# A two-layer hybrid encoder trunk: another order of the mixer's threads, and norms of two tiles in shared steps

## The chip, the cores and the metric

The kernel runs on one core of one Trainium2 chip. The metric is the device time of one execution in microseconds. The engines are named as the profile names them: PE (matrix multiplication; PEld is its loading of weights), DVE (elementwise, reductions), ACT (activation functions, copies), POOL and SP (here almost only transfers).

## What is computed

Two layers; in each a half-weighted feed-forward block, a mixer of three parts side by side, and a second feed-forward block, each behind a norm that is shifted and scaled by a conditioning vector. 256 rows (two tiles of 128), 1024 columns, float32.

```python
def dsa_attention(q, k, v, qi, ki, wi):          # queries in two blocks of 128, key chunks of 64
    # per block of queries: 8 index heads of 32
    s = einsum('bqhd,bsd->bqhs', qib, ki) * IDX_DIM ** -0.5
    idx_score = einsum('bqhs,bqh->bqs', relu(s), wib * IDX_HEADS ** -0.5)
    idx_score = where(admissible, idx_score, -inf)       # key chunk <= query chunk
    _, sel = lax.top_k(idx_score, 64)
    logits = einsum('bqhd,bqkd->bqhk', qb, k[sel]) * ATT_HEAD_DIM ** -0.5    # 8 heads of 64
    p = softmax(where(valid, logits, -inf)); o = einsum('bqhk,bqkd->bqhd', p, v[sel])

def s5_mixer(u, ...):            # 16 groups of 16 channels, 64 complex diagonal states each
    x = associative_scan(x_t = A_bar x_{t-1} + B_bar u_t)
    y = gelu(re(C x) + d_skip * u); a, g = split(y @ w_glu); return a * sigmoid(g)

def conformer_conv(h, w_dw, b_dw, ln_g, ln_b, w_pw):
    a, g = split(h); u = a * sigmoid(g)
    y = causal depthwise convolution of u, 31 taps, + b_dw
    return silu(layer_norm(y, ln_g, ln_b)) @ w_pw

def hybrid_mixer(h, w_in, w_out, ...):
    q, k, v, qi, ki, wi, u_ssm, u_conv = split(h @ w_in)
    merged = concatenate([rms_norm(dsa_attention(q, k, v, qi, ki, wi)),   # 512 columns
                          rms_norm(s5_mixer(u_ssm)),                      # 256
                          rms_norm(conformer_conv(u_conv))])              # 256
    return merged @ w_out

def reference(x, c, ...):
    for l in range(2):           # sh, sc, g: nine rows of silu(c) @ mod_w[l] + mod_b[l]
        x = x + 0.5 * g1 * swiglu_ffn(modulate(rms_norm(x), sh1, sc1), ffn1_w_gu[l], ffn1_w_down[l])
        x = x + g2 * hybrid_mixer(modulate(rms_norm(x), sh2, sc2), ...)
        x = x + 0.5 * g3 * swiglu_ffn(modulate(rms_norm(x), sh3, sc3), ffn2_w_gu[l], ffn2_w_down[l])
    return rms_norm(x, final_norm)
```

## The kernel before

Every weight matrix streams from memory once. `Stream` loads it in units of 128 x 1024 floats (`raw`) and splits each unit into a high part (ACT, L102) and a low part (DVE, L106), `hi` and `lo`; PE then makes three products per block (`mm3`, L330 to L332). Six `hi`/`lo` pairs exist; a new unit's split is issued when an older unit is done with (`st.done()`).

The feed-forward blocks are long, dense runs of such products. The mixer, which the change is about, is eight threads written as Python generators: `W` is the input projection (10 steps: tiles A, C, four of B, four of Q, which land in `ps_in`, `ps_kT`, `ps_inC`, `ps_inB`, `ps_inQ`), `K` copies keys and index queries out, `I` and `J` are the index scores and the top-k of the first and of the second tile of queries (`ps_idx`, `rl`, `idx`, then `maskb`), `S` is the state-space part (`ps_U`, `ps_V`, the scan, `ps_Y`, `ps_yT`, `ps_glu`, `ps_sg`), `C` the convolution part (`uT`, its shifted copy `U4` made by four transfers, `ps_cv`, a layer norm with `ps_cy` and `ps_cyT`, `ps_pw`), and `a` and `b` are the attention proper of the first and of the second tile (`qT`, logits `ps_lg`, softmax `Pm`, transposes `ps_PT`, products `ps_o` and `osb`). Each part's result is normed, transposed back into `ps_mg` or `ps_sg`, and split into `xTh` (ACT) and `xTl` (DVE) by `merged`; the output projection (`ps_y`) reads these. Its units come in the order of columns 4 to 7, then 0 to 3: state-space, convolution, attention.

The table `MIX_ORDER` says in which order the threads' steps are written down. A planner then places each engine's instructions in one fixed row, by readiness in its own estimate and by the order written, and every engine takes its row strictly in turn: an instruction whose operand is late holds all that stand behind it. The PSUM banks are few: two each in `ps_g` and `ps_m`, four named ones (`abank`). In the trace the profile's program names leave numbers out; `U` is both the state-space input and `U4`.

A norm needs 1/sqrt of a column of 128 values. `rsqrt_col` makes it on DVE in one guess and two refinements of three instructions each, 128x1.

## Time before, and its profile

| | us |
|---|---|
| median of 3 runs | 1192.59 |
| lowest and highest | 1190.36 and 1197.93 |
| the profiled execution | 1190.66 |
| its span, first to last instruction | 1188.9 |
| PE busy in the span | 1099.9 |
| DVE busy | 904.3 |
| ACT busy | 572.3 |
| mixer of the first layer, first input product to last output product | 286.8 to 421.8 |
| mixer of the second layer | 850.5 to 985.6 |

Times within the execution count from the span's start. 1.76 us of the profiled execution's time lie around its span. Busy shares are an average over stages; the mixers are 270 us of the span and hold all but a few instructions of the change.

### The profile page before, as it was taken

The numbers are of one execution on the slowest core, as the hardware profiler recorded it, in microseconds if no ns is written. First come the engines' busy times: TensorE is split into PE (matmuls) and PEld (weight loads), VectorE is DVE, ScalarE is ACT, GpSimd is POOL, SyncE is SP. The second block draws the span as 40 slices with busy tenths as digits, with TensorE's granted clock in tenths as the row PEclk, the third lists the DMA queues.
The fourth block names the chain that finished last, engine by engine and source line by source line (L and its number), as shares of the span: only waits on it lengthen the run. The fifth ranks groups of instructions, "written<-read, shape, count | busy, mean of one in ns | idle before, by whom it ended". The sixth has DMA issues, their size and how long they took to land. (4 is left out here: it accounts for less than half of the span.)

```text
span 1188.9 us, 19063 instructions
## 1 busy us (share of the span) xinstructions
PE 1099.9 (93%) x6915; PEld 941.3 (79%) x6915; DVE 904.3 (76%) x1806; ACT 572.3 (48%) x1032; POOL 119.2 (10%) x160
## 2 busy tenths in 40 slices
PE   3679999987989989999997999999898999999997
PEld 2558887865966869989995888888797687999986
DVE  7678999897775788898757789887677587655655
ACT  4245454445625666645445444444463566544442
POOL 7452001201012000000100000100000000000000
PEclk9789999898987999999899999999989799999999
DMA  9788988786562248678672999998456223767651
GB/s 222 188 275 278 357 290 274 234 290 182 156 147 76 72 131 301 225 236 289 205 230 89 297 330 353 318 327 263 142 156 146 69 80 120 260 198 229 199 175 54
DMA packets 189710, 251.59 MB, mean 212 GB/s; under 512 B 18886, under 2 KB 139906, under 8 KB 189616
## 3 DMA queue, kind: packets, MB, share of 16 engines
q1 hardware_dynamic: 181920, 240.56, 63.5%
q0 software_dynamic: 4704, 7.60, 2.9%
q10 hardware_dynamic: 2992, 2.22, 1.0%
q8 instruction: 54, 0.88, 0.3%
q14 instruction: 40, 0.33, 0.1%
HBM read 245.19 MB, written 1.11 MB: 207 GB/s over the span
## 5 line engine op out<-in xcount | busy, mean ns | idle before, releaser
L102 ACT ACTIVATE hi<-raw 128x1024 fp32r<-128x1024 f32 (+1 forms) x314 | 328.6, 1055 | 329.4 <-PE ps_gt L331 108.1
L106 DVE TENSOR_TENSOR lo<-raw,hi 128x1024 fp32r<-128x1024 f32 (+2 forms) x297 | 359.4, 1216 | 104.6 <-ACT hi L102 99.9
L330 PE MATMUL ps_gt<-xTh,hi 128*128 128x256 f32 x1120 | 319.0, 287 | 3.0 <-DVE h L715 2.4
L332 PE MATMUL ps_gt<-xTh,lo 128*128 128x256 f32 x1120 | 316.1, 286 | 2.2 <-DVE lo L106 2.2
L331 PE MATMUL ps_gt<-xTl,hi 128*128 128x256 f32 x1120 | 317.7, 285 | 0.0
L330 PEld LDWEIGHTS ps_gt<-xTh,hi 128*128 128x128 f32 x1120 | 215.8, 193 | 17.5 <-issue 5.9
L332 PEld LDWEIGHTS ps_gt<-xTh,lo 128*128 128x128 f32 x1120 | 215.1, 193 | 8.7 <-issue 5.0
L331 PEld LDWEIGHTS ps_gt<-xTl,hi 128*128 128x128 f32 x1120 | 216.4, 193 | 2.5 <-issue 1.7
L367 DVE SCALAR_TENSOR_TENSOR macc<-raw,cond,macc 128x512 f32<-128x512 f32 x224 | 167.0, 750 | 26.2 <-DMA raw<-in_mod_w_dram 24.8
L331 PE MATMUL ps_y<-lo,hTh 128*128 128x512 f32 x352 | 141.3, 402 | 5.2 <-DVE lo L106 5.2
L332 PE MATMUL ps_y<-hi,hTl 128*128 128x512 f32 x352 | 140.2, 398 | 1.1 <-DVE hTl L719 1.1
L330 PE MATMUL ps_y<-hi,hTh 128*128 128x512 f32 x352 | 136.4, 399 | 2.5 <-ACT hi L102 2.0
L396 POOL DMA_DIRECT2D spill<-mrow x32 | 16.2, 508 | 683.0 <-ACT mrow L393 573.4
L331 PEld LDWEIGHTS ps_y<-lo,hTh 128*128 128x128 f32 x352 | 67.9, 193 | 21.1 <-DVE lo L106 7.6
L330 PEld LDWEIGHTS ps_y<-hi,hTh 128*128 128x128 f32 x352 | 67.1, 191 | 18.2 <-ACT hi L102 3.1
L332 PEld LDWEIGHTS ps_y<-hi,hTl 128*128 128x128 f32 x352 | 67.8, 193 | 16.3 <-DVE hTl L719 1.9
L713 ACT ACTIVATE silu<-ps_gt 128x256 f32<-128x256 f32 x70 | 25.5, 377 | 50.3 <-PE ps_gt L332 49.9
L330 PE MATMUL ps_gu<-hi,xTh 128*128 128x512 f32 x96 | 40.1, 417 | 6.7 <-DVE xTh L326 6.7
L106 POOL TENSOR_TENSOR lo<-raw,hi 128x1024 fp32r<-128x1024 f32 x17 | 41.8, 2472 | 31.4 <-ACT hi L102 31.4
L332 PE MATMUL ps_gu<-hi,xTl 128*128 128x512 f32 x96 | 40.1, 417 | 3.0 <-DVE xTl L327 3.0
L715 DVE TENSOR_TENSOR h<-silu,ps_gt 128x256 f32<-128x256 f32 x70 | 28.6, 419 | 16.8 <-ACT silu L713 16.8
L331 PE MATMUL ps_gu<-lo,xTh 128*128 128x512 f32 x96 | 39.4, 410 | 0.0
(382 smaller groups left out, 1691.6 us busy)
## 6 DMA issues: line engine op xcount, KB each, us to landing
raw<-in_ffn_w_gu_dram SPq DMA_DIRECT2D x140, 512.0 KB
raw<-in_mod_w_dram SPq DMA_DIRECT2D x128, 512.0 KB
raw<-in_ffn_w_down_dram SPq DMA_DIRECT2D x88, 512.0 KB
raw<-in_ffn_w_gu_dram SPq DMA_DIRECT2D x72, 256.0 KB
raw<-in_w_in_dram SPq DMA_DIRECT2D x20, 512.0 KB
raw<-in_mod_w_dram SPq DMA_DIRECT2D x32, 256.0 KB
raw<-in_w_out_dram SPq DMA_DIRECT2D x16, 512.0 KB
row<-spill POOLq DMA_DIRECT2D x6, 512.0 KB, 4.3
```

Source lines behind the costliest of these rows:

```text
L102: nc.scalar.activation(hi[:, :n], raw[:, :n], AF.Copy)
L106: e.tensor_sub(lo[:, :n], raw[:, :n], hi[:, :n].bitcast(F32))
L330: return [nc.tensor.matmul(ps, xh, wh, start=start, stop=False), nc.tensor.matmul(ps, xh, wl, start=False, stop=False), nc.tensor.matmul(p ...
L331: nc.tensor.matmul(ps, xh, wl, start=False, stop=False),
L332: nc.tensor.matmul(ps, xl, wh, start=False, stop=stop)]
L367: nc.vector.scalar_tensor_tensor(acc, raw[:, 512 * i:512 * i + 512], cond[:, k:k + 1], prev, op0=ALU.mult, op1=ALU.add)
L396: nc.gpsimd.dma_start(d[:, 512 * h:512 * h + 512], r[32 * h:32 * h + 1, :])
L713: nc.scalar.activation(s, ps[i][:, :256], AF.Silu)
L715: nc.vector.tensor_mul(h, s, ps[i][:, 256:])
```

## The change

The table of the mixer is another one. The second tile's index scores and top-k (`J`) are written ahead of the first's (`I`), the second tile's logits (`b`) ahead of the first's (`a`) and ahead of the convolution's products, and the last steps of the state-space and convolution parts behind the attention's. The table-load for the exponential is issued after the second tile's last index scores in place of next to the keys. The two C units count as done only when `qiT` has been copied, and the splits of the units that follow are held behind that copy. The copies of `UU` are held behind the index work. `Tp`'s clearing keeps its written place. The norms of two tiles at the end of `S`, in the layer norm and at the end of `C` are made with one `rsqrt_cols` on 128x2 in place of two `rsqrt_col` on 128x1: it has four instructions in a refinement.

```diff
--- before.py
+++ after.py
@@ -44,9 +44,9 @@
 
 
 MIX_ORDER = """
-W K S K K W K J I J J I W I S J S I W I J J I S W I J I J S W C C C I J J I S W
-I J I J S I J C S W W C S W a b S N a C a C S S b b a C a b C b a a b b b C b b
-b
+W K K S K W K
+J J W J J I W J J I I S W J J I S W J J C C C W J J J S I I W I I S I I S W I I I S S W
+b a b b b b C S a a S b b C b b C S a a b a C b a C S C C
 """
 
 
@@ -265,6 +265,34 @@
             y = y2
             s = 8.0 / 3.0 * s ** 5
         return y
+
+    def rsqrt_cols(v):
+
+        def col2(tag):
+            return sm_p.tile([P, 2], F32, tag=tag, name=tag)
+        y = col2("rs2_y")
+        s = (8.0 / 3.0) ** (-6.0 / 25.0)
+        magic = float(0x5F3759DF) + math.log2(s) * float(1 << 23)
+        nc.vector.tensor_scalar(y.bitcast(I32), v.bitcast(I32), -0.5, magic, op0=ALU.mult, op1=ALU.add)
+        for _ in range(2):
+            a, b, y2 = col2("rs2_a"), col2("rs2_b"), col2("rs2_y")
+            nc.vector.tensor_mul(a, y, v)
+            nc.vector.tensor_mul(a, a, y)
+            nc.vector.scalar_tensor_tensor(b, a, -10.0 / 3.0 * s * s, a, op0=ALU.add, op1=ALU.mult)
+            nc.vector.scalar_tensor_tensor(y2, b, 5.0 * s ** 4, y, op0=ALU.add, op1=ALU.mult)
+            y = y2
+            s = 8.0 / 3.0 * s ** 5
+        return y
+
+    def rms_cols(pair, n, scale=1.0):
+
+        ss = sm_p.tile([P, 2], F32, tag="ss", name="ss")
+        for i, a in enumerate(pair):
+            j = sm_p.tile([P, 512], BF16, tag="junk", name="junk", bufs=1)
+            nc.scalar.activation(j[:, :a.shape[-1]], a, AF.Square, scale=scale * n ** -0.5, accum_out=ss[:, i:i + 1])
+        ms = sm_p.tile([P, 2], F32, tag="ms2", name="ms2")
+        nc.vector.tensor_scalar_add(ms, ss, EPS)
+        return rsqrt_cols(ms)
 
     hold = {}
 
@@ -1053,7 +1081,7 @@
                          wcol[:, n0:n0 + 16].rearrange("p (n o) -> p n o", o=1).to_broadcast([P, 16, 32]))
             yield
         Tp = T("Tp", [8, G, GC])
-        e.memset(Tp, 0.0)
+        tc.keep_in_program_order(e.memset(Tp, 0.0))
         for a in range(8):
             r = GC * (7 - a)
             nc.gpsimd.dma_start(Tp[0:P - r, a], Km[r:P])
@@ -1123,8 +1151,6 @@
                             wh, wl = us[k // 4]
                             cs = slice(256 * (k % 4) + P * j, 256 * (k % 4) + P * j + P)
                             mm3(pin["C"][:, 256 * j:256 * j + 256], wh[:, cs], wl[:, cs], *xT(k), k == 0, k == 7)
-                            if j and k % 4 == 3:
-                                st.done()
                     yield
                 else:
                     pin[i] = [bank(ps_g, f"ps_in{i}") for _ in range(2)]
@@ -1144,10 +1170,6 @@
                 ps = pin["A"][t]
                 nc.scalar.activation(vsb[:, t, :], ps[:, 8:72], AF.Copy)
                 nc.vector.tensor_scalar_mul(wis[:, t, :], ps[:, 0:8], 8 ** -0.5)
-                if t == 0:
-
-                    scr = sm_p.tile([P, 8], F32, tag="scr", name="scr", bufs=1)
-                    nc.scalar.activation(scr, ps[:, 0:8], AF.Exp)
                 yield
             pk = pin["K"][:, :256]
             for e in range(2):
@@ -1155,9 +1177,11 @@
             for b in range(4):
                 (nc.vector.tensor_copy if b % 2 else nc.scalar.copy)(kiT[32 * b:32 * b + 32], pk[64:96])
             for e in range(2):
-                nc.vector.tensor_sub(kTl[64 * e:64 * e + 64], pk[0:64], kTh[0:64].bitcast(F32))
-            yield
-            nc.scalar.activation(qiT, pin["C"], AF.Copy)
+                ktl = nc.vector.tensor_sub(kTl[64 * e:64 * e + 64], pk[0:64], kTh[0:64].bitcast(F32))
+            yield
+            st.after_hi, st.after_lo = (nc.scalar.activation(qiT, pin["C"], AF.Copy),), (ktl,)
+            st.done(2)
+            st.after_hi = st.after_lo = ()
             yield
 
         def att_index(t):
@@ -1170,14 +1194,19 @@
                     nc.tensor.matmul(ps[:, nk * i:nk * i + nk], qiT[32 * b:32 * b + 32, 256 * i + P * t:256 * i + P * t + P],
                                      kiT[32 * b:32 * b + 32, :nk], start=True, stop=True)
                 rl = s2([P, 512], "rl")
-                nc.scalar.activation(rl[:, :2 * nk], ps[:, :2 * nk], AF.Relu, scale=32 ** -0.5)
+                hold["rl"] = nc.scalar.activation(rl[:, :2 * nk], ps[:, :2 * nk], AF.Relu, scale=32 ** -0.5)
                 for i in range(2):
                     h = b + 4 * i
                     if h == 0:
                         nc.vector.tensor_scalar_mul(idx[:, :nk], rl[:, :nk], wis[:, t, 0:1])
                     else:
-                        nc.vector.scalar_tensor_tensor(idx[:, :nk], rl[:, nk * i:nk * i + nk], wis[:, t, h:h + 1],
-                                                       idx[:, :nk], op0=ALU.mult, op1=ALU.add)
+                        hold["idx"] = nc.vector.scalar_tensor_tensor(
+                            idx[:, :nk], rl[:, nk * i:nk * i + nk], wis[:, t, h:h + 1], idx[:, :nk], op0=ALU.mult, op1=ALU.add)
+                if t == 1 and b == 3:
+
+                    scr = sm_p.tile([P, 8], F32, tag="scr", name="scr", bufs=1)
+                    with tc.issue_after(hold["rl"].ins):
+                        nc.scalar.activation(scr, wis[:, 1, :], AF.Exp)
                 yield
             nc.vector.memset(idx[0:64, nk - 64:nk], NEG_INADM)
             for r in range(8):
@@ -1257,8 +1286,9 @@
             yield
             Ug = UU[32:32 + NCH, :].rearrange("c (g a j) -> c g a j", g=G, a=8)
             Ub4 = Ub.rearrange("c a (g j) -> c g a j", g=G)
-            nc.vector.tensor_copy(Ug[:, 0:8], Ub4[:, 0:8])
-            nc.scalar.activation(Ug[:, 8:16], Ub4[:, 8:16], AF.Copy)
+            with st.behind([hold["rl"], hold["idx"]]):
+                nc.vector.tensor_copy(Ug[:, 0:8], Ub4[:, 0:8])
+                nc.scalar.activation(Ug[:, 8:16], Ub4[:, 8:16], AF.Copy)
             ps = abank(0, "ps_U")
             for g in range(G):
                 nc.tensor.transpose(ps[:, NCH * g:NCH * g + NCH], Ug[:, g].rearrange("c a j -> c (a j)"), ident[32:32 + NCH, 32:32 + NCH])
@@ -1343,9 +1373,10 @@
                 nc.scalar.activation(th, pg[e][:, 256:512], AF.Tanh, scale=0.5)
                 s = s1([P, 256], F32, "ss_", "s")
                 nc.vector.scalar_tensor_tensor(s, th, 1.0, pg[e][:, 0:256], op0=ALU.add, op1=ALU.mult)
-                rs = rms_col([s], 256, 0.5)
-                nc.vector.tensor_scalar(s, s, rs, 0.5, op0=ALU.mult, op1=ALU.mult)
                 sp.append(s)
+            rs = rms_cols(sp, 256, 0.5)
+            for e in range(2):
+                nc.vector.tensor_scalar(sp[e], sp[e], rs[:, e:e + 1], 0.5, op0=ALU.mult, op1=ALU.mult)
             yield
             pt = bank(ps_m, "ps_sg")
             v = pt.rearrange("p (k n a e) -> p k e a n", k=2, a=4, e=2)
@@ -1382,20 +1413,21 @@
                 nc.scalar.activation(ya[:, ct, :], pc[:, 256 * ct:256 * ct + 256], AF.Identity, bias=col_a[:, cb + ct:cb + ct + 1])
             yield
             cg, cl = offs["ln_g"] + 2 * l, offs["ln_b"] + 2 * l
-            yn, z_ = {}, {}
+            yn, z_, pts = {}, {}, {}
+            mv = sm_p.tile([P, 2, 2], F32, tag="mv", name="mv")
             for t in range(2):
-                pt = bank(ps_m, "ps_cy")
+                pts[t] = bank(ps_m, "ps_cy")
                 for ct in range(2):
-                    nc.tensor.transpose(pt[:, P * ct:P * ct + P], ya[:, ct, P * t:P * t + P], ident)
+                    nc.tensor.transpose(pts[t][:, P * ct:P * ct + P], ya[:, ct, P * t:P * t + P], ident)
                 bs = sm_p.tile([P, 6], F32, tag="bs", name="bs")
-                mv = sm_p.tile([P, 2], F32, tag="mv", name="mv")
-                nc.vector.bn_stats(bs, pt[:, :256])
-                nc.vector.bn_aggr(mv, bs)
-                v = sm_p.tile([P, 1], F32, tag="ms", name="cv")
-                nc.vector.tensor_scalar_add(v, mv[:, 1:2], EPS)
-                rs = rsqrt_col(v)
+                nc.vector.bn_stats(bs, pts[t][:, :256])
+                nc.vector.bn_aggr(mv[:, t, :], bs)
+            v = sm_p.tile([P, 2], F32, tag="ms2", name="cv")
+            nc.vector.tensor_scalar_add(v.rearrange("p (t o) -> p t o", o=1), mv[:, :, 1:2], EPS)
+            rs = rsqrt_cols(v)
+            for t in range(2):
                 yn[t] = s1([P, 256], F32, "yn", "c")
-                nc.vector.tensor_scalar(yn[t], pt[:, :256], mv[:, 0:1], rs, op0=ALU.subtract, op1=ALU.mult)
+                nc.vector.tensor_scalar(yn[t], pts[t][:, :256], mv[:, t, 0:1], rs[:, t:t + 1], op0=ALU.subtract, op1=ALU.mult)
             yield
             for t in range(2):
                 pt = bank(ps_m, "ps_cyT")
@@ -1420,10 +1452,10 @@
                     mm3(pw[:, 256 * t:256 * t + 256], zh[:, ct, :], zl[:, ct, :], wp[0][:, cs], wp[1][:, cs], ct == 0, ct == 1)
             st.done()
             yield
+            rs = rms_cols([pw[:, 256 * t:256 * t + 256] for t in range(2)], 256)
             for t in range(2):
-                rs = rms_col([pw[:, 256 * t:256 * t + 256]], 256)
                 cm = s1([P, 256], F32, "cm", "c")
-                nc.vector.tensor_scalar_mul(cm, pw[:, 256 * t:256 * t + 256], rs)
+                nc.vector.tensor_scalar_mul(cm, pw[:, 256 * t:256 * t + 256], rs[:, t:t + 1])
                 merge(t, cm, 6, 2)
                 yield
 
```

What this does to the engines' rows, at three places of the first layer's mixer. The second layer's differ from these by a few neighbours.

First, PE where the convolution (`ps_cv`) stands. Before, among the last products of the query projection (`ps_inQ`), with 23 of them behind it:

```order
L330 MATMUL ps_inQ<-xTh,hi 128x256
L1375 MATMUL ps_cv<-U_3419,sl_W_2399 32x256 x64
L1325 MATMUL ps_yT<-ident,ye 128x4x32 x4
L331 MATMUL ps_inQ<-xTl,hi 128x256
L332 MATMUL ps_inQ<-xTh,lo 128x256
```

After, behind the whole projection, in pieces of 5, 6, 3, 5, 17, 11 and 17 among the second tile's logits (tiles 3670 and 3681 are two of its four banks):

```order
L1245 MATMUL ps_lg_3670<-maskb_3446,identb_90 128x256
L1245 LDWEIGHTS identb_90
L1245 MATMUL ps_lg_3681<-maskb_3446,identb_90 128x256
L1406 MATMUL ps_cv_3692<-U4_3403,sl_W4_2399 32x256 x5
L1335 MATMUL ps_Y_3549<-sl_O_1625,X_3506 32x128 x4
L1331 MATMUL ps_Y_3549<-sl_Tp_2474,U_3296 32x128 x4
```

The convolution moved from ahead of all logits to among them, and the last state-space products (`ps_Y`) came behind the projection too.

Second, PE at the start of the output projection (`ps_y00` is the first tile's left half; `ps_o_4093` the second tile's attention products). Before:

```order
L332 MATMUL ps_pw_3975<-hi_3653,zl_3871 128x256
L330 MATMUL ps_y00_4203<-hi_3697,xTh_112 128x512
L331 MATMUL ps_y00_4203<-lo_3698,xTh_112 128x512
L332 MATMUL ps_y00_4203<-hi_3697,xTl_113 128x512
L1239 MATMUL ps_o_4093<-vsb_2973,PT_4110 128x64 x4
L1234 MATMUL ps_PT_4155<-ident_85,Pm_3935 128x128 x4
L1239 MATMUL ps_o_4093<-vsb_2973,PT_4121 128x64 x4
L330 MATMUL ps_y00_4203<-hi_3733,xTh_112 128x512
```

After (`ps_mg_4056` holds the second tile's attention, `ps_mg_4069` the first's; all six groups of `ps_o` stand ahead of this piece):

```order
L360 MATMUL ps_pw_4082<-hi_3535,zl_4053 128x256
L1115 MATMUL ps_mg_4056<-ident_85,osb_3984 128x128 x4
L1115 MATMUL ps_mg_4069<-ident_85,osb_4006 128x128 x4
L1385 MATMUL ps_sg_4102<-ident_85,ss__3928 128x4x32 x2
L1385 MATMUL ps_sg_4102<-ident_85,ss__3932 128x4x32 x2
L358 MATMUL ps_y00_4158<-hi_3618,xTh_112 128x512
L359 MATMUL ps_y00_4158<-lo_3619,xTh_112 128x512
L358 MATMUL ps_y01_4159<-hi_3618,xTh_112 128x512
```

The output products, which were mixed with the attention's, now stand behind all of it, behind both attention transposes and the state-space transposes.

Third, ACT at the same place. Before, the merges of the state-space part (`xTh<-ps_sg`) stand among the attention's copies:

```order
L287 ACTIVATE zh_3870<-czz_3863 128x256
L1092 ACTIVATE xTh_112<-ps_sg_3922,ncol_107 128x128
L1236 ACTIVATE PT_4110<-ps_PT_4105 128x512
L1236 ACTIVATE PT_4121<-ps_PT_4116 128x512
L1092 ACTIVATE xTh_112<-ps_sg_3922,ncol_107 128x128
L277 ACTIVATE junk_4018,ss_4017<-ps_pw_3975 128x256
L102 ACTIVATE hi_4238<-raw_3657 128x1024
L277 ACTIVATE junk_4059,ss_4058<-osb_4056 128x512
```

After, they stand behind seven merges of the attention, and these behind the squares of both `osb` and of `ps_pw`:

```order
L305 ACTIVATE junk_3987,ss_3986<-osb_3984 128x512
L305 ACTIVATE junk_4009,ss_4008<-osb_4006 128x512
L315 ACTIVATE zh_4052<-czz_4045 128x256
L292 ACTIVATE junk_4116,ss_4115<-ps_pw_4082 128x256
L102 ACTIVATE hi_4193<-raw_3539 128x1024
L292 ACTIVATE junk_4118,ss_4115<-ps_pw_4082 128x256
L1120 ACTIVATE xTh_112<-ps_mg_4056,ncol_107 128x128 x3
L1120 ACTIVATE xTh_112<-ps_mg_4069,ncol_107 128x128
L1120 ACTIVATE xTh_112<-ps_mg_4056,ncol_107 128x128
L1120 ACTIVATE xTh_112<-ps_mg_4069,ncol_107 128x128 x2
L1120 ACTIVATE xTh_112<-ps_sg_4102,ncol_107 128x128
```

The first merge that the output projection reads moved from among the attention's copies to the end of the row of merges.

## Rows read from the trace of the kernel before

**Rows 1.** The page: its head, and part 1, busy time of the engines.
```profile
span 1188.9 us, 19063 instructions
...
PE 1099.9 (93%) x6915; PEld 941.3 (79%) x6915; DVE 904.3 (76%) x1806; ACT 572.3 (48%) x1032; POOL 119.2 (10%) x160
```

**Rows 2.** Stretches of the mixers: length, busy us, granted clock, DMA share, GB/s.
```profile
308.30:344.20 35.90, 35.90 (x315) 32.54 (x313) 30.11 (x68) 18.62 (x30) 1.55 (x3) 0.95 0.60 150
344.20:349.30 5.10, 0.04 (x1) 0.02 (x1) 5.03 (x21) 0.90 (x1) 0.00 (x0) 0.88 1.02 237
349.30:394.20 44.90, 44.34 (x288) 30.36 (x289) 25.24 (x91) 22.29 (x70) 9.45 (x16) 0.75 0.23 65
394.20:421.80 27.60, 27.29 (x140) 22.08 (x139) 21.49 (x71) 15.39 (x36) 0.00 (x0) 1.00 0.32 96
```

**Rows 3.** Timeline of PE: the convolution's products in each layer.
```profile
349.31 9.87 PE L1375 MATMUL ps_cv<-U,sl_W 128*32 128x256 f32 x128 [5.07 <-DMA U<-uT]
...
914.22 8.80 PE L1375 MATMUL ps_cv<-U,sl_W 128*32 128x256 f32 x128 [4.00 <-DMA U<-uT]
```

**Rows 4.** Timeline of ACT and of POOL: the shifted copy's issue and the first instruction behind it.
```profile
336.30 1.33 ACTq L1369 DMA_DIRECT2D U<-uT  x2
...
349.31 0.15 POOL L1078 MEMSET uT<- 128x60 f32 x1 [10.99 <-DMA U<-uT]
```

**Rows 5.** Stretches at the lower granted clock (columns as in Rows 2).
```profile
348.10:354.90 6.80, 5.59 (x56) 2.98 (x60) 3.65 (x20) 0.00 (x0) 2.17 (x6) 0.50 0.43 166
368.60:385.70 17.10, 17.10 (x60) 12.24 (x59) 11.78 (x43) 11.14 (x41) 1.84 (x4) 0.50 0.29 83
...
914.70:918.10 3.40, 3.40 (x40) 2.11 (x36) 1.10 (x7) 0.00 (x0) 0.00 (x0) 0.50 0.64 255
931.80:948.90 17.10, 17.10 (x56) 11.65 (x57) 11.82 (x41) 10.76 (x39) 0.57 (x1) 0.50 0.20 63
```

**Rows 6.** Timeline of PE: first products of successive heads of the second tile's logits.
```profile
379.21 0.39 PE L1216 MATMUL ps_lg<-maskb,identb 128*128 128x256 bf16 x1
...
380.26 0.39 PE L1216 MATMUL ps_lg<-maskb,identb 128*128 128x256 bf16 x1
...
387.73 0.27 PE L1216 MATMUL ps_lg<-maskb,identb 128*128 128x256 bf16 x1
...
388.37 0.28 PE L1216 MATMUL ps_lg<-maskb,identb 128*128 128x256 bf16 x1
```

**Rows 7.** Timeline of DVE: both masks made; what it next waits for.
```profile
351.36 0.42 DVE L1189 TENSOR_SCALAR maskb<-idx 128x128 bf16<-128x128 f32 x2
360.59 0.69 DVE L296 TENSOR_TENSOR yT<-ps_yT,yT 64x512 fp32r<-64x512 f32 x1 [8.80 <-ACT yT L295]
```

**Rows 8.** Instructions on `osb`, `zh` and `ps_pw`: duration ns min/median/max, first and last start.
```profile
L1243 DVE TENSOR_TENSOR osb<-ps_o,rin x4: 691/692/693, 388.0 to 963.0; 128x512 f32<-128x512 f32 x4
L277 ACT ACTIVATE junk<-osb x4: 630/639/647, 396.2 to 963.8; 128x512 bf16<-128x512 f32 x4
...
L287 ACT ACTIVATE zh<-czz x4: 417/432/445, 389.1 to 955.9; 128x256 fp32r<-128x256 f32 x4
L288 DVE TENSOR_TENSOR zl<-czz,zh x4: 418/424/426, 390.0 to 956.4; 128x256 fp32r<-128x256 f32 x4
...
L277 ACT ACTIVATE junk<-ps_pw x4: 383/390/396, 394.9 to 962.8; 128x256 bf16<-128x256 f32 x4
```

**Rows 9.** Timeline of ACT: a unit's split, and two merges one behind the other.
```profile
395.23 1.08 ACT L102 ACTIVATE hi<-raw 128x1024 fp32r<-128x1024 f32 x1
...
401.35 0.37 ACT L1092 ACTIVATE xTh<-ps_mg,ncol 128x128 fp32r<-128x128 f32 x1 [0.61 <-PE ps_mg L1087]
402.13 0.37 ACT L1092 ACTIVATE xTh<-ps_mg,ncol 128x128 fp32r<-128x128 f32 x1 [0.42 <-DVE xTl L1093]
```

**Rows 10.** Timeline of DVE: one step of a norm's refinement.
```profile
395.77 0.22 DVE L262 SCALAR_TENSOR_TENSOR rs_a<-rs_y,ms 128x1 f32<-128x1 f32 x1
```

**Rows 11.** Timeline of PE: a group of transposes of `osb` into `ps_mg`.
```profile
402.34 0.60 PE L1087 MATMUL ps_mg<-ident,osb 128*128 128x128 f32 x4
```

## The prediction, on record before the changed kernel ran

> **What bounds the kernel now.** I read the page first. PE is busy for 1099.9 us of the span of 1188.9 us [rows 1], so time is won or lost where PE idles, runs at the lower clock, or is asked for other work. The change asks for no other work: its products are the same, in another order. Next I cut the first layer's mixer into stretches [rows 2]. From 308.3 to 344.2 PE is busy throughout. Then comes a stretch of 5.1 us with 0.04 us of PE. In the 44.9 us behind it PE is busy but for 0.6 us, at a mean granted clock of 0.75, and in the last 27.6 us but for 0.3 us, at full clock. So there are two things to win in this mixer: the one hole, and the low clock. The timeline names the hole: the convolution's first products wait 5.07 us in the first layer and 4.00 us in the second for the shifted copy of `uT`, a transfer [rows 3]. It is issued from 336.3 us on and has landed at 349.3 us, 13.0 us later [rows 4]. The stretches at half clock (0.50, the 1.2 GHz level) are two in each layer: 6.8 and 3.4 us around that hole, and 17.1 us over the last gate products, the first tile's logits and half of the second's [rows 5]. Last I asked whether the top-k holds anything up. Both masks are made by 351.8 us, and DVE then idles 8.80 us [rows 7], since PE is at the convolution; the top-k is not what PE waits for.
>
> The sum is made against the profiled execution's 1190.66 us, which lies 1.93 us under the median of the three runs.
>
> **The hole, and the conv's low clock.** With the convolution behind the 23 query products and among logits, PE reaches it about where it reaches it now: 23 products more ahead of it at 35.9/315 = 0.11 us each are 2.6 us, and 60 short state-space products leave for some 2 us; an estimate of 345 us. The copy's issue comes earlier. Before, the B products that feed it were mixed with the state-space products (`ps_U`, `ps_V`); now those stand behind all of B, and 49 short products at about 0.11 us are 5 to 6 us. So the issue falls near 330.5 us, and by the old 13.0 us the copy lands near 343.5 us. That hides the wait with a margin of 1 to 2 us: -5.1 and -4.0 us. If the transfer takes longer, what is over the margin comes back. The convolution itself took 9.87 us with 5.6 us of it at half clock, and 8.80 us with 3.4 us; taking half of each off gives 7.07 and 7.10 us, so a product here takes just twice as long at half clock. Without the hole ahead, I count -2.8 and -1.7 us. Sum so far: -13.6 us.
>
> **The long stretch at half clock.** At half clock a head of the second tile's logits takes 380.26 - 379.21 = 1.05 us, at full clock 388.37 - 387.73 = 0.64 us [rows 6]: 39% of the time is lost, 6.7 us of each 17.1 us. What ran when the clock fell was the gate products, without any idling of PE. The new order has the first tile's logits and the gate products again in one run. I carry the stretch over unchanged: 0 us. The bounds are -6.7 us a layer (it doesn't fall) and +2.7 us (it falls 7 us earlier, at the first tile's logits).
>
> The Trainium skill, in "TensorE: Matmul & The Clock Gate" under Terms, prices throttled time at its length times the share of clock withheld, which is half. The convolution's two lengths agree with that; the logits' 39% doesn't. By the rule each long stretch costs 8.6 us in place of 6.7; since I leave it as it is, the sum is the same by either, and the rival below that loses the stretch would give 1180 us.
>
> **The start of the output projection.** Here the new order costs. Before, output products begin at 394 us among the attention's products, and PE never idles for long [rows 2]. Now PE's row has all `ps_o` first, then `ps_pw`, both attention transposes, the state-space transposes, and only then the first output product; and ACT's row has the state-space merges behind seven attention merges. From the first tile's last `ps_o` to the first output product, step by step: `osb` 0.69, its square 0.64, `zh` behind it on ACT 0.43, `zl` 0.42 [rows 8], two `ps_pw` products about 0.3, the square of `ps_pw` 0.39, a unit's split standing in ACT's row 1.08 [rows 9], the second square 0.39. The transposes of `osb` (0.60 [rows 11]) are done by then. Then four merges of the bank that the state-space transposes need, each 402.13 - 401.35 = 0.78 us, since ACT's next waits for DVE's half of the last [rows 9]: 3.1. Then two short transposes, about 0.5, and a merge, 0.37. With ten hand-offs of about 0.05 us this is 8.8 us. PE's own work in it is 8 `ps_pw` products (about 1.0), two groups of 0.60 and the state-space pair (0.4), together 2.6 us. It idles 6.2 us. Ahead of it `ps_o` waits for copies of `ps_PT` that stand in ACT's row among four steps of the layer norm and `zh`; I put 1.3 us on that, three merges' worth of ACT. Together +7.5 us a layer. Bounds: 5.0 us, if the merges of two banks alternate and cost 0.37 each and half of the split is hidden; 9.5 us, if `osb` waits its turn on DVE.
>
> Behind such an idle stretch I expect PE at half clock again, as around the hole: there it cost 2.8 and 1.7 us. I take the mean, 2.25 us a layer; bounds 0 and 3.4 (half of 6.8). Together the new start costs 15.0 + 4.5 = +19.5 us.
>
> **The rest.** The second tile's logits now start some 17 us sooner and wait for `qT`, which ACT and DVE make right behind the projection; PE has convolution products to fill with. I put 0.5 us a layer on it, between 0 and 2: +1.0 us. The second tile's mask has to be made by 345 us. DVE is busy 30.1 of 35.9 us in that stretch [rows 2], but the first tile's top-k and the scan now stand behind it, so I expect it near 335 us: 0 us, and what it would be late is what PE would wait. The splits that are held behind `qiT` start later, but PE has 48 products of two ready units, 5.5 us, ahead of the first that needs them: 0 us, and up to 2 us if the cover is thin. The shared norms save six short instructions of at most 0.22 us [rows 10], 1.3 us of DVE, at three places in each layer; DVE isn't waited for at two of them, and at the last the attention's merges stand ahead in any case: 0 us, at best -1 us a layer. The table-load, the held `UU` copies and the clearing of `Tp` move on engines with idle time to cover them (ACT 18.6 of 35.9 us busy [rows 2]): 0 us; without that cover the state-space products come later, which stand behind the projection now. SP's row of loads is as before, so no transfer of weights moves ahead of another.
>
> **Sum.** -13.6 + 0 + 19.5 + 1.0 = +6.9 us, on 1190.66 us: 1197.6 us.
>
> **The rivals.** First, *the clock stays up* (faster). The long stretch goes, because convolution and logits are now mixed and the gate products stand alone. For it: the clock rose again at 385.7 us while logits, transposes and attention products went on. Against it: it fell in the midst of gate products that are the same now. It gives 1197.6 - 13.4 = 1184.2 us, and with the short start below it passes the mark for faster. Second, *a short start*: ACT is ahead of its row and the output products start 2.5 us sooner, without the low clock: -5.0 - 4.5, 1188.1 us. For it speaks that ACT is busy only 22.3 of 44.9 us [rows 2]; against it, that the chain is made of hand-offs, not of load. Third, *the clock stays down* (slower): from the first tile's logits through the gate products, and over the idle start of the output projection, PE is at half clock without a break. That doubles the 17.1 us, at 39% another 6.7 us a layer: 1197.6 + 13.4 = 1211.0 us. It decides from about the point at which two thirds of that come true. Its place is between the end of `ps_cv` and the tenth output product. Fourth, *the hole stays*: the copy lands later than 345 us, because ACT issues two of its four transfers behind the copies of `UU` and `U`. Then PE waits at the first pieces of the convolution instead, up to the old 9.1 us: 1206.7 us.
>
> **How the numbers follow.** One per cent, 11.9 us, is about what a measurement of this kernel can tell from no change. Forecast 0.42, clock up 0.17, short start 0.13, clock down 0.18, hole stays 0.10. The low end is the clock up with 2 us less of a start, 1182 us; the high end the forecast with the upper bounds of the start (4.0) and of the stretch (5.4), 1207 us, with 1 us for the copy: 1208 us. Faster by over 1% takes the clock up and something of the short start: 0.18. Slower takes most of the third and fourth and the forecast's upper edge: 0.29. Within 1%: 0.53.
>
> **What would show it.** In the changed kernel's trace the first `ps_cv` should have no idle time from a transfer; the mixer's PE should idle 5 to 9 us, in few pieces, between the last `ps_o` and the first output products, and start these at a granted clock of 0.5; a stretch of about 17 us at 0.5 should lie over the gate products. I am wrong if output products start within 3 us of the last `ps_o`, if no half clock lies over `ps_glu`, or if `ps_cv` waits.

## The result and the profile of the changed kernel

The changed kernel takes 1203.57 us (median of four runs, 1201.25 to 1208.59), the kernel before 1191.47 us beside it (four, 1187.28 to 1197.93): 1.0101 times as long, 95% interval 1.0059 to 1.0144. The forecast of 1197.6 us is 6 us short of it, inside its range. The profiled execution took 1201.25 us, with a span of 1199.5 us against 1188.9 [rows 1]. Ratios and their intervals, here and below, leave out executions that took over 1.5% longer than the fastest of their kernel; medians are over all executions.

First three stretches of the span: the first mixer, what lies between the mixers, and the second mixer. After the length come the busy times of PE, PEld, DVE, ACT and POOL, each with its number of instructions, then the granted clock, the DMA share and GB/s. The kernel before:

```profile
286.80:421.80 135.00, 125.92 (x866) 101.74 (x867) 98.48 (x285) 72.88 (x167) 12.24 (x22) 0.90 0.44 116
421.80:850.50 428.70, 415.74 (x2603) 363.23 (x2600) 345.85 (x592) 208.43 (x344) 24.21 (x43) 0.98 0.78 254
850.50:985.60 135.10, 127.36 (x866) 104.20 (x867) 97.08 (x280) 73.10 (x166) 2.75 (x5) 0.89 0.42 114
```

The changed kernel:

```profile
285.50:430.30 144.80, 135.39 (x866) 109.22 (x867) 96.87 (x266) 74.30 (x167) 11.69 (x20) 0.85 0.40 108
430.30:853.70 423.40, 409.82 (x2604) 357.83 (x2602) 347.71 (x594) 208.72 (x345) 25.60 (x43) 0.99 0.79 257
853.70:996.30 142.60, 133.89 (x866) 109.08 (x867) 96.10 (x262) 73.75 (x166) 2.76 (x5) 0.84 0.39 108
```

The mixers are 9.8 and 7.5 us longer, the stretch between them 5.3 us shorter, the head 1.3. In the mixers PE runs the same 866 products. Its idle time (length less busy) went from 9.08 to 9.41 us and from 7.74 to 8.71: +1.3 us in all. Its busy time went up by 9.47 and 6.53 us, at a mean granted clock of 0.85 and 0.84 in place of 0.90 and 0.89. So the idle time in the main changed its place, and the rest is busy time on the same products. Part of that is the lower clock. Another part is the convolution: it now runs at full clock, but in pieces among the logits, and keeps PE busy for 9.98 and 8.14 us, where one unbroken run of the same 128 products took 7.11 us at full clock (the experiment on the hole, below). PE's `ps_cv` alone, in each layer:

```profile
348.50:368.00 19.50, 9.98 (x128) 1.00 0.20 60
915.00:935.00 20.00, 8.14 (x128) 1.00 0.17 54
```

The hole of [rows 3] is gone: in PE's timeline the line of the convolution's first products has no bracket, so PE did not wait for them.

```profile
348.82 0.83 PE L1406 MATMUL ps_cv<-U,sl_W 128*32 128x256 f32 x9
```

The shifted copy is issued at 329.4 us and has landed when POOL, which waits for it, goes on (timelines of ACT and of POOL, for [rows 4]):

```profile
329.43 1.35 ACTq L1400 DMA_DIRECT2D U<-uT  x2
...
342.67 0.16 POOL L1106 MEMSET uT<- 128x60 f32 x1 [11.20 <-DMA U<-uT]
```

The idle time is now at the start of the output projection. PE's timeline of the first layer, from the first tile's last `ps_o` on:

```profile
394.28 1.10 PE L1268 MATMUL ps_o<-vsb,PT 128*128 128x64 f32 x8
...
397.45 0.38 PE L358 MATMUL ps_pw<-hi,zh 128*128 128x256 f32 x1 [1.54 <-ACT zh L315]
...
399.15 1.11 PE L1115 MATMUL ps_mg<-ident,osb 128*128 128x128 f32 x4 [0.50 <-DVE osb L1275]
402.47 1.11 PE L1115 MATMUL ps_mg<-ident,osb 128*128 128x128 f32 x4 [2.21 <-DVE osb L1275]
404.76 0.69 PE L1385 MATMUL ps_sg<-ident,ss__3928 128*128 128x128 f32 x2 [1.18 <-DVE xTl L1121]
...
406.46 0.80 PE L358 MATMUL ps_y<-hi,xTh 128*128 128x512 f32 x1 [0.58 <-ACT xTh L1120]
```

The five brackets add up to 6.0 us; in the second layer the five of the same place give 6.3. The first output product starts 11.1 us behind the last `ps_o`. In ACT's timeline the first two merges of a bank stand 1.43 us apart, where [rows 9] had 0.78:

```profile
400.43 0.37 ACT L1120 ACTIVATE xTh<-ps_mg,ncol 128x128 fp32r<-128x128 f32 x1
401.86 0.37 ACT L1120 ACTIVATE xTh<-ps_mg,ncol 128x128 fp32r<-128x128 f32 x1 [1.07 <-DVE xTl L1121]
```

DVE's half of the first merge (`xTl`) comes late, since the low part of a unit's split stands in DVE's row ahead of it:

```profile
400.20 1.23 DVE L106 TENSOR_TENSOR lo<-raw,hi 128x1024 fp32r<-128x1024 f32 x1 [0.34 <-ACT hi L102]
...
401.48 0.35 DVE L1121 SCALAR_TENSOR_TENSOR xTl<-ps_mg,ncol,xTh 128x128 fp32r<-128x128 f32 x1
```

The four transposes took 0.60 us in [rows 11] and take 1.11 here, at half clock: 46% of the longer time is lost to it. The stretches at half clock in the changed kernel:

```profile
317.20:320.60 3.40, 3.40 (x17) 3.17 (x15) 1.24 (x3) 1.34 (x2) 0.00 (x0) 0.50 0.99 386
327.40:334.20 6.80, 6.80 (x40) 6.74 (x40) 6.56 (x22) 1.52 (x4) 1.42 (x2) 0.50 0.65 136
337.70:341.10 3.40, 3.40 (x17) 3.40 (x17) 1.60 (x4) 1.53 (x3) 0.00 (x0) 0.51 0.69 81
371.80:392.30 20.50, 20.50 (x70) 15.02 (x70) 8.55 (x35) 8.40 (x22) 4.01 (x6) 0.50 0.25 71
399.10:409.30 10.20, 6.18 (x19) 4.43 (x20) 7.96 (x32) 5.42 (x17) 0.00 (x0) 0.50 0.16 51
...
935.00:958.90 23.90, 23.90 (x76) 16.67 (x77) 9.47 (x36) 9.94 (x28) 0.57 (x1) 0.50 0.21 66
969.10:975.90 6.80, 5.11 (x14) 3.85 (x15) 4.96 (x21) 3.41 (x10) 0.00 (x0) 0.50 0.25 77
```

Against [rows 5], the one at `ps_cv` is gone, the long one is 20.5 and 23.9 us in place of 17.1, and one over the first output products is new. The first layer's projection holds three, 13.6 us in all. It held one before, which [rows 5] doesn't show, and so did the second layer's:

```profile
320.80:324.20 3.40, 3.40 (x17) 3.22 (x17) 3.14 (x7) 1.49 (x3) 0.00 (x0) 0.50 0.00 0
884.00:890.80 6.80, 6.80 (x28) 5.64 (x27) 4.98 (x9) 3.12 (x5) 0.13 (x1) 0.50 0.08 33
```

### The profile page after: what moved, and what is told of

Its sections match the earlier page's. It is cut to its first block, busy times and chain, and to the rows that moved or that the text cites. A ratio compares the mean times of both kernels' runs of the same rounds, so it can differ in the third digit from the quotient of the medians.

```text
span 1199.5 us, 19036 instructions
## 1 busy us (share of the span) xinstructions
PE 1106.7 (92%) x6915; PEld 946.9 (79%) x6915; DVE 901.6 (75%) x1770; ACT 575.2 (48%) x1032; POOL 119.7 (10%) x160
## 3 DMA queue, kind: packets, MB, share of 16 engines
HBM read 245.19 MB, written 1.11 MB: 205 GB/s over the span
## 4 chain that ended last, share of the span: by engine, by line
PE 75%; DVE 11%; DMA 6%; issue 4%; ACT 3%; SPq 1%; DVEq 0%; ACTq 0%
PE ps_gt L358 10%; PE ps_gt L359 10%; PE ps_gt L360 10%; PE ps_y L360 7%; PE ps_y L358 7%; PE ps_y L359 7%; DMA raw<-in_ffn_w_gu_dram 3%; DMA raw<-in_mod_w_dram 3%; DVE lo L106 2%; DVE macc L395 2%; PE ps_mod L419 2%; PE ps_gu L358 2%; PE ps_gu L360 2%; PE ps_gu L359 2%; PE ps_cv L1406 1%
## 5 line engine op out<-in xcount | busy, mean ns | idle before, releaser
L358 PEld LDWEIGHTS ps_y<-hi,hTh 128*128 128x128 f32 x352 | 66.0, 188 | 16.8 <-ACT hTh L746 2.8
L743 DVE TENSOR_TENSOR h<-silu,ps_gt 128x256 f32<-128x256 f32 x70 | 28.5, 416 | 16.8 <-ACT silu L741 16.7
```

Source lines behind the costliest of these rows:

```text
L358: return [nc.tensor.matmul(ps, xh, wh, start=start, stop=False), nc.tensor.matmul(ps, xh, wl, start=False, stop=False), nc.tensor.matmul(p ...
L743: nc.vector.tensor_mul(h, s, ps[i][:, 256:])
```

## The experiments

The theory: the new late half of the table starts the output projection late, and costs more, with the low clock there, than the closed hole returns. The rivals: the new early half costs it, by a low clock over the projection; or the small edits (splits, `UU` copies, shared norms) do. Ratios are to the kernel before, measured beside it on the same chip, with their 95% intervals. The kernels were measured on several chips, so two of them are best compared by their ratios.

| kernel | median us | ratio |
|---|---|---|
| changed kernel | 1203.57 | 1.0101 (1.0059 to 1.0144) |
| new order, none of the edits | 1214.51 | 1.0178 (1.0132 to 1.0223) |
| edits, old order | 1189.58 | 0.9969 (0.9930 to 1.0009) |
| old early, new late half | 1201.88 | 1.0059 (1.0017 to 1.0102) |
| new early, old late half | 1190.64 | 1.0007 (0.9978 to 1.0035) |
| the same, `ps_pw`'s norm by tile | 1192.97 | 1.0005 (0.9968 to 1.0043) |
| before, hole closed | 1190.48 | 0.9986 (0.9940 to 1.0032) |
| the same with the edits, `ps_pw`'s norm by tile | 1190.89 | 0.9971 (0.9937 to 1.0005) |
| changed, state-space merge early | 1195.17 | 1.0012 (0.9971 to 1.0053) |
| the same, `ps_pw`'s norm by tile | 1193.44 | 1.0000 (0.9964 to 1.0036) |
| merge early, convolution's part last | 1182.72 | 0.9881 (0.9836 to 0.9927) |

### Both kernels once more

No edit.

> The kernel before once more, unchanged, for a second profile. If the order alone sets where PE's clock is low, the half clock in the mixers is again 27 and 31 us, each within 3.4 us, and the stretch between the mixers is again 428 to 429 us. If it is chance from one execution to the next, one of the three differs by more than 6 us of half clock, or 4 us of time.

> The changed kernel once more, unchanged, for a second profile. If the order alone sets where PE's clock is low, the half clock in the mixers is again 44 us each, within 3.4 us, and the stretch between the mixers 423 us. If it is chance, one of the three differs by more than 6 us of half clock, or 4 us of time; the idle time at the start of the output projection (6.0 and 6.3 us) should repeat within 0.5 us in either case.

They took 1192.07 and 1202.35 us. Each mixer is cut where the convolution or the logits begin: its front is the projection with the index work, its back all behind that. The kernel before in its two profiles (first mixer's front and back, then the second's):

```profile
286.80:349.30 62.50, 54.29 (x441) 49.30 (x442) 51.76 (x125) 35.19 (x63) 2.79 (x6) 0.96 0.63 161
349.30:421.80 72.50, 71.63 (x425) 52.44 (x426) 46.72 (x162) 37.69 (x104) 9.45 (x16) 0.84 0.26 77
850.60:914.20 63.60, 56.78 (x441) 51.64 (x442) 51.14 (x126) 35.41 (x63) 2.19 (x4) 0.92 0.59 151
914.20:985.60 71.40, 70.53 (x425) 52.51 (x426) 45.84 (x155) 37.59 (x103) 0.57 (x1) 0.86 0.26 82
```

```profile
285.80:349.90 64.10, 56.73 (x445) 51.90 (x446) 51.19 (x121) 35.19 (x63) 4.32 (x7) 0.92 0.60 152
349.90:421.10 71.20, 70.33 (x425) 51.34 (x426) 47.41 (x165) 37.75 (x104) 9.45 (x16) 0.86 0.27 82
846.60:915.20 68.60, 61.04 (x445) 55.48 (x446) 51.69 (x128) 35.50 (x63) 2.19 (x4) 0.83 0.56 140
915.20:987.00 71.80, 70.94 (x425) 51.84 (x426) 45.38 (x153) 37.64 (x103) 0.57 (x1) 0.85 0.25 81
```

And the changed kernel:

```profile
285.50:348.50 63.00, 59.59 (x409) 54.83 (x409) 50.92 (x127) 33.91 (x61) 2.37 (x6) 0.89 0.61 160
348.50:430.30 81.80, 75.79 (x460) 54.40 (x459) 45.95 (x141) 40.38 (x107) 9.31 (x14) 0.81 0.23 68
853.70:915.10 61.40, 59.00 (x408) 54.65 (x408) 48.28 (x114) 33.87 (x61) 2.19 (x4) 0.89 0.63 165
915.10:996.30 81.20, 74.89 (x460) 54.43 (x459) 47.82 (x149) 39.88 (x106) 0.57 (x1) 0.81 0.21 65
```

```profile
286.90:345.40 58.50, 55.09 (x408) 50.39 (x408) 48.31 (x121) 33.63 (x60) 2.30 (x6) 0.97 0.63 164
345.40:429.70 84.30, 77.77 (x460) 55.45 (x459) 48.50 (x147) 40.47 (x108) 9.29 (x14) 0.80 0.25 71
854.80:916.20 61.40, 59.01 (x408) 54.67 (x408) 48.27 (x114) 33.83 (x61) 2.18 (x4) 0.89 0.61 165
916.20:997.50 81.30, 75.00 (x460) 54.52 (x459) 47.81 (x149) 39.82 (x106) 0.57 (x1) 0.81 0.22 65
```

The backs repeat: 71.2 to 72.5 us before, 81.2 to 84.3 us after, at a clock of 0.84 to 0.86 and of 0.80 to 0.81. The fronts don't: with one order, 63.6 us at 0.92 and 68.6 us at 0.83 in the second layer before, 63.0 us at 0.89 and 58.5 us at 0.97 in the first after. So the low clock over the projection changes by chance (the second of the two outcomes put down for each kernel), while that in the back repeats: by lengths and clocks it is 20 to 23 us at half clock in the four backs before, and 31 to 34 us after. Half clock there is no full account of the cost, though: the kernel with the hole closed and the edits (below) has as much of it, backs of 72.5 us at 0.79 and 75.1 us at 0.77, at a ratio of 0.9971. The stretch between the mixers is chance too: 428.7 and 425.5 us before, 423.4 and 425.1 after. The idle time at the start of the output projection repeats: 5.98 and 6.31 us in the second profile, as in the first. On the means of the two profiles the backs cost +10.4 us a layer (71.7 to 82.1), and the fronts give -3.6 (64.7 to 61.1). The 35 more products in the back are mostly short state-space ones.

### The order alone, and the edits alone

```diff
 # first kernel: the kernel before, with the changed table
-W K S K K W K J I J J I W ... a b b b C b b b
+W K K S K W K J J W J J I W ... b a C b a C S C C
 # second kernel: the changed kernel, with the table of before
-W K K S K W K J J W J J I W ... b a C b a C S C C
+W K S K K W K J I J J I W ... a b b b C b b b
-            with st.behind([hold["rl"], hold["idx"]]):
+            (the copies of UU not held)
```

> The kernel before with only the new order of the threads' steps; the norms, the splits, the copies of UU, the table load and the clearing of Tp stay as they were. Theory (the order is the cost: output products start late, some 6 us of PE idle a layer at it, and the clock is low over more of each mixer): 1.01 times before, about 1203 us, like the changed kernel, with first output products some 11 us behind the last ps_o of the first tile. Rival (the small edits are the cost, by splits held behind qiT and UU copies held behind the index): the order alone wins what the hole was worth, 0.99, about 1180 to 1185 us. A third possibility concerns the stretch between the two mixers, which became 5.4 us shorter: if the order did that, it is about 423 us here too, and if the clearing of Tp did, it is about 429 us and the kernel is nearer to 1208 us.

> The changed kernel with the order of before, and with the UU copies not held; what is left of the change is the shared norms, the splits behind qiT, the moved table load and the clearing of Tp in program order. Theory: within 3 us of before (ratio 0.9975 to 1.0025), with the hole of 5.1 and 4.0 us ahead of ps_cv still there. Rival (small edits cost): 1.005 to 1.01. If the clearing of Tp shortens the stretch between the mixers by 5 us, the ratio is 0.995.

The cost is the order's: without the edits it is even higher, 1.0178, and 1214.51 us where about 1203 were expected. There the copy of `uT` is issued at 339.5 us in place of 329.4, and the convolution waits 1.52 and 1.55 us. So the edits help the new order by an earlier copy at least; how much of the 0.8% between the two kernels is clock by chance stays open. The edits alone can't be told from no change. The hole is still there (5.53 and 4.38 us), as expected, and the stretch between the mixers was 429.4 us: the clearing of `Tp` doesn't shorten it. Nor does the order: with the order alone it was 422.6 us, but it was as short in the kernel before with the hole closed.

### The halves of the table crossed

The early half is what stands up to the end of the projection.

```diff
 # changed kernel, late half of before
-b a b b b b C S a a S b b C b b C S a a b a C b a C S C C
+C S C a b S a C a C S S b b a C a b C b a a b b b C b b b
 # changed kernel (UU copies not held), early half of before but for the convolution's products; late half new
-W K K S K W K J J W J J I W ... J J J S I I W I I S I I S W I I I S S W
+W K S K K W K J I J J I W I S J S I W I J J I S W I J I J S W C C C I J J I S W I J I J S I J S W W W
```

> The changed kernel with only the late half of the table (all behind the projection) put back to the order of before; the early half (second tile's index and top-k first, state-space part behind it, convolution's products behind the query products) stays changed. Theory (the late half is the cost, by the start of the output projection): PE idles under 2 us a layer behind the first ps_o, the half clock over the output products goes, and the hole stays closed: 10 to 18 us under the changed kernel, 1186 to 1194 us, ratio to before 0.995 to 1.002. Rival (the early half is the cost, by the half clock over the projection, 13.7 us a layer against 4.6 and 10.2): still 1.005 or more, 1198 us and up.

> The other cell: the early half in the order of before (UU copies not held), with the convolution's products and its later steps in the new late half. Theory: output products start 8 to 11 us behind the last ps_o of the first tile with about 6 us of PE idle a layer and half clock behind it, 10 to 15 us over the kernel with the hole closed (1190.5 us): 1200 to 1206 us, ratio 1.007 to 1.013. Rival (early half is the cost): 1188 to 1194 us, 0.997 to 1.002.

The old late half takes the changed kernel back to 1190.64 us, and the new late half costs with the old early half too, 1201.88 us (1.0059, a little less than the 1.007 to 1.013 expected; its profiled execution was the longest of its ten, so only its waits are read: 1.97, 3.02 and 0.46 us ahead of the first output product). The late half is the cost, and the first rival falls as the main cause: with either late half, the new early half stands 0.4% above the old one (1.0101 and 1.0059; 1.0007 and 0.9969 for the edits in the old order), which these intervals can't tell from nothing. But two expectations failed: I expected under 2 us of idle time with the old late half and no half clock behind it. PE waited 4.21 us in each layer, with 3.4 and 6.8 us at half clock behind the waits:

```profile
406.63 0.44 PE L1115 MATMUL ps_mg<-ident,cm 128*128 128x128 f32 x2 [4.21 <-DVE cm L1458]
...
964.30 0.69 PE L1115 MATMUL ps_mg<-ident,cm 128*128 128x128 f32 x2 [4.21 <-DVE cm L1458]
```

`cm` is the convolution's normed output, whose norm two tiles now share.

The crossing also shows that the late start isn't the whole cost of the late half. In the two mixers together PE idles 16.3 us with the old late half and 18.1 us in the changed kernel, nearly as long; but it is busy 261.1 us in place of 269.3. Some of that is the convolution, which the old late half runs ahead of the logits, 7.7 us in each layer in place of 9.98 and 8.14. The rest of this busy time was not taken apart.

### That norm for each tile by itself

```diff
-            rs = rms_cols([pw[:, 256 * t:256 * t + 256] for t in range(2)], 256)
             for t in range(2):
+                rs = rms_col([pw[:, 256 * t:256 * t + 256]], 256)
```

> The kernel with the changed early half and the late half of before (1190.6 us), with the norm of ps_pw taken for each tile by itself again, as before the change; the other two norms stay shared. Theory (the shared norm of ps_pw is what holds its output products up, 4.2 us in each layer by the wait for cm): that wait falls to under 1 us, 7 to 10 us less, 1181 to 1184 us, ratio to before 0.990 to 0.994, and this beats both kernels. Rival (ps_pw itself ends too late, so the first tile's cm is late either way): 3 us or more of the wait stays, 1188 to 1191 us, 0.997 or more.

The waits at `cm` fell, but to 2.05 and 1.14 us, each with 1.14 us more for its merge behind it:

```profile
399.11 0.44 PE L1115 MATMUL ps_mg<-ident,cm 128*128 128x128 f32 x2 [2.05 <-DVE cm L1458]
400.69 0.80 PE L358 MATMUL ps_y<-hi,xTh 128*128 128x512 f32 x1 [1.14 <-ACT xTh L1120]
```

Of 4.2 us 1.0 and 1.9 are won, and no time that can be measured: a ratio of 1.0005 against 1.0007. Neither expectation is met in full: 3.2 and 2.3 us of waiting are left, where the theory had under 1 and the rival 3 or more. The ratio is as the rival said (0.997 or more).

### The hole alone

```diff
 # the kernel before
-... I J I J S I J C S W W C S W a b S N ...
+... I J I J S I J S W W S W C C a b S N ...
```

> The kernel before with one step moved: the convolution's products stand behind the last of the query products (and its next step behind the gate products' place), all else as before. The sum of the prediction prices this at 9.1 us for the wait and 4.5 us for the low clock: 1178 us, ratio 0.989. Rival (the clock falls elsewhere in place of it, so only the idle time is won): 1182 to 1183 us, 0.992 to 0.993. If the copy is late even so, or the convolution's later steps become what the output projection waits for: 0.997 to 1.003.

> The order of before with the convolution's products moved behind the query products (0.9986 alone) and the change's small edits (0.9969 alone), except that the norm of ps_pw is taken for each tile by itself and the UU copies are not held. Theory (both add up): 1184 to 1188 us, 0.993 to 0.9965. Rival (what the hole gives back goes to waits for ps_PT and to low clock elsewhere, whatever the small edits are): 1189 to 1193 us, 0.997 to 1.001.

The second adds the change's edits to the first, with the norm of `ps_pw` by tile and the `UU` copies not held. Neither wins more than 0.3%, with intervals that reach 1: of the outcomes put down, the third came for the first kernel and the rival's for the second. In the first kernel the copy still lands at 349 us, so 2.26 and 0.42 us of the wait are left; the logits, now in one run, leave PE waiting for `Pm`:

```profile
909.42 7.11 PE L1375 MATMUL ps_cv<-U,sl_W 128*32 128x256 f32 x128 [0.42 <-DMA U<-uT]
937.79 2.16 PE L1234 MATMUL ps_PT<-ident,Pm 128*128 128x128 f32 x7 [1.01 <-ACT Pm L1224]
```

The convolution itself took 7.11 us, as the prediction had it at full clock. What closing the hole returns didn't show in the time: the intervals leave room for a gain of some 7 us at most, where 13.6 were summed up. PE's idle time in the mixers fell from 16.8 to 13.1 us only, since 2.7 us of the old wait are left and the backs idle 2.8 us more.

### The start of the output projection

First the state-space merge, the last `S`, is moved ahead of the attention's merges; then the norm is split again; then the output products are taken in another order.

```diff
-... C b b C S a a b a C b a C S C C
+... C b b C S a a S b a C b a C C C
 # third kernel, beside it
-OUT_ORDER = [4, 5, 6, 7, 0, 1, 2, 3]
+OUT_ORDER = [4, 5, 0, 1, 2, 3, 6, 7]
```

> The changed kernel with one step moved: the state-space merge (the thread's last step) stands ahead of the attention merges and of ps_pw, so the first output products, which read the state-space part, can run while the attention merges are made. Theory: PE's idle time between the last ps_o and the output products falls from 6.0 and 6.3 us to 1 to 2 us a layer, and the half clock behind it (10.2 and 6.8 us) goes or shrinks: 10 to 18 us less than the changed kernel, 1186 to 1194 us, ratio to before 0.995 to 1.002. Rival (what is late is the attention and convolution merges, so the idle time only moves behind the first 24 output products): no more than 3 us less a layer, 1198 to 1203 us.

> The changed kernel with the state-space merge moved early (1195.2 us; it left waits for cm of 5.2 and 4.9 us) and the norm of ps_pw taken for each tile by itself again. Theory (the shared norm holds cm up): the waits fall to 1 to 2.5 us, 5 to 8 us less, 1187 to 1190 us, ratio 0.996 to 0.998. Rival (the convolution's steps stand too late in the order, so cm waits for ps_pw and its squares either way): the waits stay over 4 us, 1193 to 1197 us.

> The changed kernel with the state-space merge moved early (1195.2 us) and the output products taken in the order state space, attention, convolution in place of state space, convolution, attention; their weights come in that order too. Theory (PE idles for want of the convolution's parts, while the attention's of the first tile are ready): the waits for cm of 5.2 and 4.9 us fall under 1.5 us each, 6 to 9 us less, 1186 to 1190 us, ratio 0.995 to 0.998. Rival (any gain of idle time goes to a lower clock, as in the kernels before this one, where mixers with less idle time had more half clock): the waits go, and the time stays within 3 us of 1195.

With the merge early the first output product starts at 397.26 us, right at the last `ps_o`, in place of 406.46. The kernel is faster, by 8 us or 0.9%, but not for the reason given: after 18 output products of the state-space part PE has nothing, since the convolution's part comes next:

```profile
404.01 0.60 PE L1115 MATMUL ps_mg<-ident,osb 128*128 128x128 f32 x4
409.82 1.08 PE L1115 MATMUL ps_mg<-ident,cm 128*128 128x128 f32 x4 [5.21 <-DVE cm L1458]
```

The idle time has moved, as the rival had it: the backs idle 5.6 and 6.5 us, where the changed kernel's idle 6.0 and 6.3. By its ratio the time is the theory's (0.995 to 1.002), but what makes it shorter is not shown. With a norm for each tile the waits are still 3.30 and 4.86 us, and the time is within its noise (1.0000 against 1.0012). With the convolution's part last they are gone. PE's timeline shows one wait in the first layer from the last `ps_o` to the end of the mixer, and in the second 1.38 us ahead of the first output product and 0.43 us later. The one of the first layer, and the mixers' fronts and backs:

```profile
391.60 0.50 PE L358 MATMUL ps_y<-hi,xTh 128*128 128x512 f32 x1 [0.84 <-ACT xTh L1120]
```

```profile
285.10:342.20 57.10, 54.48 (x409) 50.57 (x410) 48.37 (x121) 33.73 (x61) 2.31 (x6) 0.97 0.63 168
342.20:415.40 73.20, 71.64 (x460) 49.73 (x459) 47.97 (x146) 39.95 (x108) 9.31 (x14) 0.88 0.28 82
839.10:902.40 63.30, 60.17 (x409) 56.13 (x409) 48.34 (x114) 34.03 (x61) 2.19 (x4) 0.87 0.61 160
902.40:977.10 74.70, 72.58 (x460) 52.27 (x459) 48.07 (x149) 39.29 (x106) 0.57 (x1) 0.84 0.23 71
```

The backs are 73.2 and 74.7 us with the same 460 products that took 81.2 to 84.3, at a clock of 0.88 and 0.84. The convolution is still in pieces here, 9.98 and 8.14 us. This kernel takes 1182.72 us: 1.2% under the kernel before, and faster than both. The gain over the kernel with the early merge, 12.5 us by the medians and 1.3% by the ratios, is more than the 6 to 9 us expected, and the rival (idle time turns into low clock) falls: with the waits, the low clock over the output products went too (with the early merge 3.4 us of it in the first layer and 10.2 in the second, here none).

## Why the prediction was right, point by point

The forecast was right as a whole, because its main cost was: the new start of the output projection outweighs the closed hole. That its number came within 6 us of the median is in part luck, as the terms show:

- **The hole, -9.1 us.** Right: issue at 329.4 us (330.5 said), landing at 342.7 (343.5 said). The margin was 6 us, not 1 to 2, since PE came to the convolution at 348.8 us. In the second profile, with a clock of 0.97 in front, PE came at 345.75 and the copy had landed at 344.19: 1.6 us, as said.
- **The conv's low clock, -4.5 us.** Wrong. The low clock left the convolution, and the convolution got hardly shorter: 9.98 and 8.14 us in pieces at full clock, where it took 9.87 and 8.80 in one run with part of it at half clock: -0.6 us. The sum priced it at 7.07 and 7.10 us although it put it among logits, and had no term for the pieces. Half clock also comes and goes in the fronts by chance: 13.6 us of it lay over the first projection in one profile of the changed kernel, 3.4 us in the other.
- **The long stretch, 0.** Its place was right, over the gate products, and its size wrong. It was 20.5 and 23.9 us long, in both profiles, where 17.1 were carried over (the prediction counted two stretches in each layer and passed over those in the projection): 3.4 and 6.8 us more, at 46% (1.11 against 0.60 us) about 1.6 and 3.1 us.
- **The start of the output projection, +15.0 us.** The idle time was 6.0 and 6.3 us where 6.2 was worked out. The 1.3 us a layer for `ps_o` waiting on its copies did not come, 2.6 us too much. Nor were the 0.87 us taken off that PE had idled in each back before. So the backs' idle time grew by 10.6 us, not 15.0. The chain was longer than 8.8 us, 11.1 in the first layer: half clock stretched the PE work in it, and the split in DVE's row held a merge up, which the term had not.
- **Half clock behind it, +4.5 us.** 6.18 and 5.11 us of PE's work lay in it; at 46% that is some 2.8 and 2.4 us, 5.2 in all.
- **The rest.** The second tile's mask is made at 335.4 us, as said. The logits' wait for `qT`, +1.0 us, didn't come (0.36 us in the second profile's first layer); the held `UU` copies made PE wait 0.57 and 0.50 us for `ps_U`, which had been put at 0. No wait for `cm` shows in this order, so the shared norm of `ps_pw` cost nothing there; with the old late half it was on the path, as the crossed kernels show.

By the first profile: idle time +1.3 us where the terms give -9.1 + 15.0 + 1.0 = +6.9, busy time in the mixers +16.0 where they give 0, outside them -6.7 where they give 0; together +10.6. Too much idle time, and a stretch between the mixers that came out short by chance, stood against busy time that had no term. In the mixers' stretches at half clock PE was busy 79.6 us in place of 53.4; at the 39% of the logits to the 46% of the transposes, the 26.2 us more make an estimated 10 to 12 of the 16.0 us. The convolution's pieces, 18.1 us in place of 14.2 at full clock, make up to 4 us (their ends overlap the logits between them). The weak steps are thus the clock, taken from one profile of before as if the order alone set it, and the convolution's price among logits. On two profiles of each kernel about half of the +10.4 us in each back is idle time (6.0 to 6.5 us against 0.9), and the other half busy time, of which the shares of clock and of pieces weren't measured apart.

Of the rivals, a start without the low clock and a hole that stays are refuted by the trace. The clock that stays up didn't come. The one that stays down came in part: 20.5 and 10.2 us, with 6.8 us at full clock between them, in the first layer.

The rule of the Trainium skill, "TensorE: Matmul & The Clock Gate", Terms (throttled time costs its length times the withheld share, one half), lies near these transposes' 46% and above the logits' 39%.

## What to carry to other kernels

Set the order of an engine's work from its consumer: here the output projection asked for state space, convolution, attention, while the attention's part was ready before the convolution's. Moving one producer forward only moved PE's wait to the next part; taking the parts in the order in which they become ready removed it, and was worth 1.3% against the kernel with the producer moved. Price a run of short products again when it is to be cut into pieces: here the convolution's pieces kept PE busy for 18.1 us at full clock, where the unbroken runs took 18.7 with part of them at half clock. Before a low clock of one profile is counted as gain or loss, take a second profile of the same kernel, and count only what repeats.

## What the runs showed of the hardware

Where PE runs at half clock differs from one execution to the next with the same instructions: one front took 63.6 and 68.6 us, at mean clocks of 0.92 and 0.83 (the two executions may be of two chips). The spread of the runs goes with it, on one chip too: among 21 runs of the kernel before the shortest span was 1183.9 us, at a mean clock of 0.956, and the longest 1199.7 us, at 0.942. That 1.3% between executions is as large as the change that was to be measured.

The convolution's 128 products kept PE busy for 7.11 us in one run, and for 9.98 and 8.14 us in pieces among logits and state-space products, all at full clock.
